# Reading both halves of an input-projection chunk out of their PSUM bank at the chunk's end

## The chip, the cores and the metric

The kernel runs on one core of a Trainium2 chip. The metric is the device time of one execution in microseconds (us); all times here come from the profiled execution or from timed runs of the same program. Engine names are those of the profile: PE multiplies matrices, PEld loads its weights, DVE (VectorE) and ACT (ScalarE) do the element-wise work, POOL is GpSimd, SP issues most transfers.

## What is computed

One layer on 256 tokens of width 1024, in float32: a wide input projection, a recurrent branch (RWKV-7) and a causal attention branch from its columns, a gated mix, a layer norm, and a mixture of 32 experts with the top 4 per token.

```python
proj = x @ w_in                                            # 256 x 5408
sh = token_shift(proj[..., :SHIFT_COLS], mu_shift)         # t + (previous token - t) * mu
y_rwkv = rwkv7_time_mix(r, k, v, ... of sh)
y_attn = moba_attention(q, k, v of proj)                   # rope on q and k, causal softmax
mixed = sigmoid(gate_a) * (y_attn @ w_attn_br) + sigmoid(gate_r) * (y_rwkv @ w_rwkv_br)
h = layer_norm(ALPHA * x + mixed @ w_out)
out = layer_norm(ALPHA * h + moe_ffn(h, ...))              # 32 experts, w1 1024 x 2048, w2 1024 x 1024
```

## The kernel before

**The input projection in chunks and units.** Twenty chunks of 256 columns of `w_in` (numbered 1 to 20) are multiplied with the activations. A chunk's weights come in with one transfer of 1 MB (`load`, L112), and `split` (L121) turns them into a high and a low part with two ACT casts (L128) and two DVE subtractions (L129) of 128x1024 each. A chunk has two halves: of 128 columns each in `proj_shift` and `proj_gate`, of 128 tokens each in `proj_tok`. A half is eight units, one per slice of the contraction, and a unit is three matmuls of 128x256 (`mm3`, L133; lines L135 to L137). So a chunk is 16 units and the projection 320, counted here from 0: chunk c is units 16(c-1) to 16c-1. Both halves lie in one 2 KB PSUM bank, and chunks take banks 0 and 1 in turn.

**How the chunks are read.** Chunks 1 to 6 (k, r, v of the recurrent branch): `shift` (L204), one ACT operation (L205) and one DVE operation (L206) per half. Chunks 7 and 8 (values of attention): one ACT copy per half (L258). Chunks 9 to 12 and 17 to 20 (the two gates): one ACT sigmoid per half (L245). Chunks 13 to 16 (q and k of attention): `rope`, four DVE operations per half (L271, twice L274, L276).

**What sets the order.** PE runs in program order, written by hand. `units()` (L248) is a generator of the 320 units; between the steps of the recurrent branch and of attention the program takes some of them as filler with `fill(n)` or `fill_to(n)`. The order of ACT, DVE, SP and POOL is made by a scheduler when the program is built, and each of these engines then works through its list in order. Waits between engines are placed when the program is built, too.

**The steps around the units that the prediction names**, in program order: the small projections and exponentials of the recurrent branch (L298 to L404); four products that fill the matrices AT (L423), with two units after each; the inversion of triangular blocks on DVE (31 steps, L481 and L483), whose result goes through DRAM and comes back with eight transfers on ACT's queue (L508) for the matmuls of L518 and L526 (after unit 207); the recurrence over four blocks of 64 tokens c = 0 to 3, each a chain of PE and DVE steps (L570, L571, L577, L578, L585, L592, L598, L602) with 10 units between them; two group norms (L538, L551); the transposes of q and k (L626); attention: `scores(0)`, 18 units, `scores(1)`, 12 units, `turn_scores(0)` (L664), units to 313, `weigh(0)` (L677), units to 319. A `scores` step has its softmax on DVE and ACT (exponentials L654, last multiplication L658).

**After unit 319**: the products with the branch and output matrices, the second norm and the router, then a loop over 32 experts whose weights (12 MB each) are streamed by SP (L733) into eleven buffers of 2 MB and one shared with other tiles. A transfer starts when PE has used the buffer's former content (`mdone`). Several of these buffers hold tiles of the projection and of attention before; the transfers of the first experts start when those are done (`mfill`, from L766).

Of the kernel before, what the change touches and what calls it, by code (L numbers as in the profile page):

```python
# [13 lines left out]
AF = mybir.ActivationFunctionType  # L14
# [48 lines left out]
def hybrid_kernel(ctx, tc, xt_d, x_d, win_d, w0_d, ups_d, up2_d, par_d, cA_d, cB_d, wbr_d, wout_d,  # L63
# [7 lines left out]
    V, A, PE, G = nc.vector, nc.scalar, nc.tensor, nc.gpsimd  # L71
# [23 lines left out]
    def bank(i, shape=(512,)):  # L95
        cnt[0] += 1
        return psum.tile([128] + list(shape), FT, name=f"b{i}_{cnt[0]}", tag=f"b{i}")
# [23 lines left out]
    def split(n):  # L121

        if n >= len(chunks):
            return
        hl = pair(hls[n % 3], FR)
        for q in range(2):
            c = slice(1024 * q, 1024 * q + 1024)
            A.copy(hl[:, 0, c], RAW[n][:, c])  # L128
            V.tensor_tensor(hl[:, 1, c], RAW[n][:, c], hl[:, 0, c].bitcast(FT), op=OP.subtract)  # L129
        HL[n] = hl.rearrange("p x (a b) -> p x a b", a=8 if chunks[n][0] == "in" else 4)  # L130
        load(n + 2)

    def mm3(ps, lhs, rhs, first, last):  # L133

        PE.matmul(ps, lhs[0], rhs[0], start=first, stop=False)  # L135
        PE.matmul(ps, lhs[0], rhs[1], start=False, stop=False)  # L136
        PE.matmul(ps, lhs[1], rhs[0], start=False, stop=last)  # L137
# [66 lines left out]
    def shift(dst, ps, mc, m=128):  # L204
        A.activation(dst, ps, AF.Copy, scale=par[:m, P_OM + mc:P_OM + mc + 1])  # L205
        V.scalar_tensor_tensor(dst[:, 1:T], ps[:, 0:T - 1], par[:m, P_MU + mc:P_MU + mc + 1], dst[:, 1:T],  # L206
                               op0=OP.mult, op1=OP.add)
# [7 lines left out]
    def proj_shift(n, b, dst, f0, mc):  # L215
        split(n + 2)
        ps = bank(b, (2, T))
        for h in range(2):
            for kt in range(8):
                mm3(ps[:, h], [HL[n][:, x, kt, 128 * h:128 * h + 128] for x in range(2)], (xh[:, kt], xl[:, kt]),  # L220
                    kt == 0, kt == 7)
                if kt == 7:
                    shift(dst[:, f0 + h], ps[:, h], mc + h)
                yield

    def proj_tok(n, b, done):
        split(n + 2)
        ps = bank(b, (2, 256))
        for tt in range(2):
            tk = slice(128 * tt, 128 * tt + 128)  # L230
            for kt in range(8):
                mm3(ps[:, tt], (xh[:, kt, tk], xl[:, kt, tk]), [HL[n][:, x, kt] for x in range(2)], kt == 0, kt == 7)
                if kt == 7:
                    done(tt, ps[:, tt])
                yield

    def proj_gate(n, b, dst):
        split(n + 2)
        ps = bank(b, (2, T))
        for h in range(2):  # L240
            for kt in range(8):
                mm3(ps[:, h], [HL[n][:, x, kt, 128 * h:128 * h + 128] for x in range(2)], (xh[:, kt], xl[:, kt]),
                    kt == 0, kt == 7)
                if kt == 7:
                    A.activation(dst[:, h], ps[:, h], AF.Sigmoid)  # L245
                yield

    def units():  # L248
        yield from proj_shift(1, 0, k, 0, 4)
        yield from proj_shift(2, 1, k, 2, 6)  # L250
        yield from proj_shift(3, 0, r, 0, 0)
        yield from proj_shift(4, 1, r, 2, 2)
        yield from proj_shift(5, 0, v, 0, 8)
        yield from proj_shift(6, 1, v, 2, 10)

        for half in range(2):
            yield from proj_tok(7 + half, half,
                                lambda tt, ps: A.copy(va_tok[:, tt, 256 * half:256 * half + 256], ps))  # L258
        G_["A"] = slot(15, [8, T])
        for j in range(4):  # L260
            yield from proj_gate(9 + j, j % 2, G_["A"][:, 2 * j:2 * j + 2])
# [18 lines left out]
        for u in range(4):  # L280
            yield from proj_tok(13 + u, u % 2, rope(*divmod(u, 2)))
        G_["R"] = slot(9, [8, T])
        for j in range(4):
            yield from proj_gate(17 + j, j % 2, G_["R"][:, 2 * j:2 * j + 2])
# [59 lines left out]
    for f in range(4):  # L344
        c = slice(128 * f, 128 * f + 128)
        if f % 2 == 0:
            ps = bank(6 + f // 2, (2, T))
# [27 lines left out]
    for f2 in range(2):  # L375
        ps = bank(3 + f2, (2, T))
# [40 lines left out]
    for c in range(4):  # L417
        tt, pr = divmod(c, 2)
# [6 lines left out]
        for h in range(2):  # L425
            ps = pss[h]
# [17 lines left out]
    for c in range(4):  # L444
        ps = bank(2 + c)
# [16 lines left out]
    for tt in range(2):  # L462
        ps = bank(4 + tt)
# [14 lines left out]
    for j in range(31):  # L478
# [5 lines left out]
        if j < 4:  # L484
            c = j
            tt, pr = divmod(c, 2)
            hk, hn = slice(64 * pr, 64 * pr + 64), slice(64 - 64 * pr, 128 - 64 * pr)
            ps = bank(2 + c)
# [72 lines left out]
    for c in range(4):  # L561
        tt, pr = divmod(c, 2)
# [17 lines left out]
        if c < 3:  # L580
            ph = bank(5, (4, 128))
            for s in range(8):
                f, h = s % 4, s // 4
# [12 lines left out]
        for s in range(8):  # L596
            f, h = s % 4, s // 4
# [24 lines left out]
    for f in range(4):  # L622
        ps = bank(6 + f % 2, (2, T))
# [144 lines left out]
    for br, (ys_, gt) in enumerate(((yRs, gR), (yAs, gA))):  # L768
        for cc in range(2):
# [7 lines left out]
            for dd in range(2):  # L777
                d2 = 2 * cc + dd
                ps = bank(2 + d2, (2, T))
# [165 lines left out]
    ps = bank(5, (4, E))  # L945
# [88 lines left out]
    def first(e, b):  # L1034
        j = e % 2
        ps = bank(4 + b)
        pick = misc.tile([128, 128], FR, name="pick", tag="pick")
        A.activation(pick, bo, AF.Copy, scale=dup[:, 2 * e + b:2 * e + b + 1])
        for x in range(2):
            PE.matmul(ps, pick, b1r[:, x], start=x == 0, stop=False)  # L1040
        for kt in range(8):
            w = MW[e, 4 * b + kt // 2]
            for g_ in range(2):
                PE.matmul(ps[64 * g_:64 * g_ + 64], XG[:, kt, 64 * j:64 * j + 64],  # L1044
                          w[:, kt % 2, 512 * g_:512 * g_ + 512], start=False, stop=kt == 7)
            if kt % 2:
                mdone((e, 4 * b + kt // 2))
        return ps
# [32 lines left out]
    for e in range(E):  # L1081
# [6 lines left out]
        ps = first(e, 0)  # L1088
# [125 lines left out]
    with tc.manual_schedule(engines={mybir.EngineType.PE}):  # L1214
        second(E - 2, lambda: turn(E - 1, (1,)))
        for n in range(2):
            ps = [bank(4 + 2 * n + a) for a in range(2)]
# [89 lines left out]
```

## Time and profile before

| | us |
|---|---|
| median of 3 runs (lowest, highest) | 1246.01 (1243.99, 1248.87) |
| profiled execution | 1243.01 |
| its span, first to last instruction | 1241.2 |
| PE, DVE, ACT busy | 1133.4, 387.4, 285.6 |

The profiled execution lies 3.0 us below the median of the runs and has 1.8 us outside its span. Two parts follow each other: the front, up to about 317 us, in which the projection, the two branches and the router run, and the expert loop, from there to the end. In a row of a timeline an idle time and what ended it stand in brackets.

### The profile page before, as it was taken

To read this page: it belongs to the slowest core of one execution; us is meant where nothing else is said; L and a number is where in the kernel's file an instruction comes from. 1 tells how busy PE (TensorE), PEld (TensorE's weight loads), DVE (VectorE), ACT (ScalarE), POOL (GpSimd) and SP (SyncE) were. 2 spreads that over 40 slices of the span, in tenths; PEclk is the share of its full clock that TensorE was granted. 3 is DMA by queue.
4 is the path that set the end of the run, shared out by engine and by line. 5 is a ranking of instruction groups with operands and counts; after the bars stand their busy time and mean duration, and the time that the engine had idled before them with its cause. 6 is when DMAs were issued, how large, how long until landed. Compare 5 with 4: busy or idle time off the path is not lost.

```text
span 1241.2 us, 15213 instructions
## 1 busy us (share of the span) xinstructions
PE 1133.4 (91%) x6434; PEld 596.0 (48%) x6434; DVE 387.4 (31%) x809; ACT 285.6 (23%) x577; POOL 6.5 (1%) x16
## 2 busy tenths in 40 slices
PE   8889887799999999999998989898999999999976
PEld 6678776798444343444433333343343333334322
DVE  4778466465222221222222121211121112222113
ACT  5534325444111111111111111111111111121112
POOL 0000000000000000000000000000000000000000
PEclk9999988899899999999999999999999999999997
DMA  7335423399699999999999999999999999999992
GB/s 269 106 116 156 150 94 145 135 364 380 264 429 427 428 427 429 427 427 418 426 426 430 426 427 429 428 426 428 427 428 427 429 427 428 427 427 427 428 414 87
DMA packets 45549, 441.02 MB, mean 355 GB/s; under 512 B 13010, under 2 KB 13538, under 8 KB 17954
## 3 DMA queue, kind: packets, MB, share of 16 engines
q1 hardware_dynamic: 36002, 436.93, 84.8%
q10 hardware_dynamic: 9472, 3.05, 1.1%
q8 instruction: 52, 0.85, 0.3%
q14 instruction: 23, 0.19, 0.0%
HBM read 438.13 MB, written 1.84 MB: 354 GB/s over the span
## 4 chain that ended last, share of the span: by engine, by line
DMA 49%; PE 41%; DVE 5%; ACT 4%; issue 1%; ACTq 0%; SPq 0%; DVEq 0%
DMA both<-in_w_dram 31%; DMA q<-in_w_dram 16%; PE b L1044 13%; PE b L1027 7%; PE b L135 4%; PE b L137 3%; PE b L136 3%; PE b L914 2%; DVE q L129 1%; PE b L1040 1%; ACT q L128 1%; DMA both<-in_win_dram 1%; PE b L1009 1%; PE b L1064 1%; ACT both L654 1%
## 5 line engine op out<-in xcount | busy, mean ns | idle before, releaser
L1044 PE MATMUL b<-both,s 128*64 128x512 f32 x1280 | 289.8, 600 | 20.4 <-DMA both<-in_w_dram 20.3
L1044 PEld LDWEIGHTS b<-both,s 128*64 128x64 f32 x1280 | 87.8, 138 | 204.7 <-issue 163.2
L1044 PE MATMUL b<-q,s 128*64 128x512 f32 x752 | 171.3, 601 | 4.0 <-DMA q<-in_w_dram 3.8
L1053 DVE TENSOR_SCALAR s<-b 128x256 f32<-128x256 f32 x64 | 27.2, 425 | 440.7 <-PE b L1044 440.7
L1027 PE MATMUL b<-both,s 128*64 128x512 f32 x576 | 128.9, 595 | 3.4 <-DMA both<-in_w_dram 3.4
L135 PE MATMUL b<-q,q 128*128 128x256 f32 x320 | 99.4, 311 | 33.4 <-ACT both L245 15.3
L1027 PE MATMUL b<-q,s 128*64 128x512 f32 x416 | 96.7, 612 | 8.5 <-DMA both<-in_w2l_dram 7.4
L1044 PEld LDWEIGHTS b<-q,s 128*64 128x64 f32 x752 | 51.2, 138 | 107.8 <-issue 97.6
L1069 ACT COPY s<-b 128x256 f32<-128x256 f32 x64 | 23.7, 371 | 323.0 <-PE b L1064 241.1
L137 PE MATMUL b<-q,q 128*128 128x256 f32 x320 | 93.5, 292 | 0.8 <-DVE q L129 0.8
L136 PE MATMUL b<-q,q 128*128 128x256 f32 x320 | 93.5, 292 | 0.0
L1017 DVE TENSOR_TENSOR s<-b,s 64x512 fp32r<-64x512 f32 (+1 forms) x66 | 44.4, 673 | 129.2 <-ACT s L1016 126.8
L135 PEld LDWEIGHTS b<-q,q 128*128 128x128 f32 x320 | 64.3, 201 | 41.0 <-ACT both L245 16.7
L1016 ACT CAST s<-b 64x512 fp32r<-64x512 f32 (+1 forms) x66 | 37.5, 568 | 191.2 <-PE b L1027 178.6
L1027 PEld LDWEIGHTS b<-both,s 128*64 128x64 f32 x576 | 40.4, 137 | 79.5 <-issue 77.8
L914 PEld LDWEIGHTS b<-s,s 128*128 128x128 f32 x512 | 61.7, 200 | 13.8 <-issue 13.0
L914 PE MATMUL b<-s,s 128*128 128x128 f32 x512 | 65.0, 287 | 1.4 <-DVE rt L958 0.7
L137 PEld LDWEIGHTS b<-q,q 128*128 128x128 f32 x320 | 64.3, 201 | 1.0 <-DVE q L129 1.0
L136 PEld LDWEIGHTS b<-q,q 128*128 128x128 f32 x320 | 64.7, 202 | 0.2 <-issue 0.2
L1054 ACT ACTIVATE s<-s 128x256 f32<-128x256 f32 x64 | 27.0, 421 | 143.8 <-DVE s L1053 143.8
L1027 PEld LDWEIGHTS b<-q,s 128*64 128x64 f32 x416 | 29.6, 140 | 62.4 <-issue 59.9
L129 DVE TENSOR_TENSOR q<-both,q 128x1024 fp32r<-128x1024 f32 x44 | 52.5, 1218 | 16.9 <-ACT q L128 16.6
(294 smaller groups left out, 1078.2 us busy)
## 6 DMA issues: line engine op xcount, KB each, us to landing
both<-in_w_dram SPq DMA_DIRECT2D x116, 2048.0 KB, 39.1
q<-in_w_dram SPq DMA_DIRECT2D x73, 2048.0 KB, 39.1
both<-in_win_dram SPq DMA_DIRECT2D x19, 1024.0 KB, 5.1
both<-in_wout_dram SPq DMA_DIRECT2D x4, 1024.0 KB, 7.2
both<-in_w2l_dram SPq DMA_DIRECT2D x7, 512.0 KB, 25.9
s<-in_wbr_dram SPq DMA_DIRECT2D x2, 1024.0 KB, 6.2
both<-in_wbr_dram SPq DMA_DIRECT2D x2, 1024.0 KB, 4.9
s<-in_w_dram SPq DMA_DIRECT2D x2, 1024.0 KB, 16.0
```

The lines of the kernel that those rows point to most:

```text
L129: V.tensor_tensor(hl[:, 1, c], RAW[n][:, c], hl[:, 0, c].bitcast(FT), op=OP.subtract)
L135: PE.matmul(ps, lhs[0], rhs[0], start=first, stop=False)
L136: PE.matmul(ps, lhs[0], rhs[1], start=False, stop=False)
L137: PE.matmul(ps, lhs[1], rhs[0], start=False, stop=last)
L914: PE.matmul(pg[d // 4][:, d % 4], xtok[:, tt, 128 * d:128 * d + 128], oh[:, tt], start=tt == 0 and d % 4 == 0, stop=tt == 1 and d % 4 == 3)
L1016: A.copy(hi, ps)
L1017: V.tensor_tensor(lo, ps, hi.bitcast(FT), op=OP.subtract)
L1027: PE.matmul(ps[64 * n:64 * n + 64], aTs[e % 2][:, b, hf, 64 * g_:64 * g_ + 64], w[:, hf, 512 * n:512 * n + 512], start=ft == 0, stop=ft == 7)
L1044: PE.matmul(ps[64 * g_:64 * g_ + 64], XG[:, kt, 64 * j:64 * j + 64], w[:, kt % 2, 512 * g_:512 * g_ + 512], start=False, stop=kt == 7)
L1053: V.tensor_scalar(gl, pv[:, :, 0], 7.0, None, op0=OP.min)
L1054: A.activation(sw, gl, AF.Sigmoid, scale=1.702)
L1069: A.copy(aTs[e % 2][:, b], ps[:, 2 * i:2 * i + 2])
```

## The change

In all three helpers the reading of half 0 moves from unit 7 of the chunk to unit 15, where half 1 is read too. The condition `h + kt == 8` holds once in a chunk, at h = 1 and kt = 7. The two shifts, and the two calls of `done`, follow each other; the two sigmoids of 128x256 become one of 128x512. No matmul, transfer or buffer changes, and the units are yielded as before.

```diff
@@ proj_shift
-                if kt == 7:
-                    shift(dst[:, f0 + h], ps[:, h], mc + h)
+                if h + kt == 8:
+
+                    for hh in range(2):
+                        shift(dst[:, f0 + hh], ps[:, hh], mc + hh)
                 yield
@@ proj_tok
-                if kt == 7:
-                    done(tt, ps[:, tt])
+                if tt + kt == 8:
+                    for t2 in range(2):
+                        done(t2, ps[:, t2])
                 yield
@@ proj_gate
-                if kt == 7:
-                    A.activation(dst[:, h], ps[:, h], AF.Sigmoid)
+                if h + kt == 8:
+                    A.activation(dst, ps, AF.Sigmoid)
                 yield
```

## Rows read from the trace of the kernel before

**Rows 1.** The chain that ended last, 1150 us to the end: start, us, what
```profile
1162.76 40.83 DMA q<-in_w_dram
```

**Rows 2.** Stretches: busy PE, PEld, DVE, ACT, POOL, then PEclk, DMA share, GB/s
```profile
310.00:320.00 10.00, 9.25 (x47) 7.15 (x47) 2.71 (x14) 1.98 (x5) 0.00 (x0) 0.67 0.53 227
...
340.00:350.00 10.00, 10.00 (x50) 3.44 (x46) 2.01 (x6) 0.98 (x3) 0.00 (x0) 1.00 1.00 429
```

**Rows 3.** Waits of SP, 60 to 400 us: total us, times, longest
```profile
SPq L733 <- PE b L1044: 58.8, 10, 17.8
```

**Rows 4.** The same view, the first 144 us of the front
```profile
0.00:144.00 144.00, 123.52 (x920) 109.39 (x921) 94.27 (x170) 65.94 (x104) 3.62 (x14) 0.98 0.52 164
```

**Rows 5.** Waits of PE, 0 to 144 us: total us, times, longest
```profile
PE b L135 <- DVE both L206: 5.4, 3, 2.2
PE b L135 <- DVE s L206: 3.6, 2, 2.5
PE b L135 <- DVE both L274: 3.2, 1, 3.2
PE b L135 <- ACT both L245: 2.6, 4, 1.2
...
PE b L465 <- DVE s L206: 0.9, 1, 0.9
...
PE b L135 <- ACT both L258: 0.5, 1, 0.5
```

**Rows 6.** Waits of PE, 144 to 201 us
```profile
PE b L135 <- DVE both L274: 4.6, 3, 2.1
PE b L577 <- DVE both L571: 2.8, 1, 2.8
```

**Rows 7.** Waits of PE, 201 to 260 us
```profile
PE b L135 <- ACT both L245: 12.7, 3, 6.1
```

**Rows 8.** Timeline of PE: units 40, two of chunk 18, and unit 280
```profile
47.88 0.39 PE L135 MATMUL b<-q,q 128*128 128x256 f32 x1
...
210.08 0.28 PE L135 MATMUL b<-q,q 128*128 128x256 f32 x1
...
210.44 0.28 PE L135 MATMUL b<-q,q 128*128 128x256 f32 x1
...
217.05 0.58 PE L135 MATMUL b<-q,q 128*128 128x256 f32 x1 [6.09 <-ACT both L245]
```

**Rows 9.** Busy time and granted clock of two stretches (columns as Rows 2)
```profile
170.00:178.00 8.00, 8.00 (x67) 7.59 (x68) 3.03 (x7) 0.82 (x2) 0.00 (x0) 0.58 0.01 2
...
215.00:222.00 7.00, 4.95 (x25) 4.77 (x26) 2.59 (x3) 1.97 (x3) 0.00 (x0) 0.57 0.47 161
```

**Rows 10.** Groups by form, 0 to 260 us: count, busy us, mean ns, idle
```profile
L668 ACT COPY both<-b 128x512 f32<-128x512 f32 x4 | 2.3, 586 | 5.9 <-PE b L664 5.9
...
L206 DVE SCALAR_TENSOR_TENSOR both<-b,par,both 128x255 f32<-128x255 f32 x10 | 4.7, 477 | 8.6 <-ACT both L205 8.5
```

**Rows 11.** Timeline of DVE: a rope half, a step of the recurrence, the softmax's last
```profile
152.35 0.42 DVE L271 TENSOR_TENSOR both<-b,both 128x256 f32<-128x256 f32 x1 [0.21 <-PE b L137]
...
153.20 0.42 DVE L276 TENSOR_TENSOR both<-both 128x256 f32<-128x256 f32 x1
...
183.11 0.67 DVE L571 TENSOR_TENSOR both<-b,both 64x512 f32<-64x512 f32 x1
...
215.24 1.22 DVE L658 TENSOR_TENSOR both<-both,smst 128x1024 f32<-128x1024 f32 x1
```

**Rows 12.** Timeline of ACT around the first softmax
```profile
209.46 1.28 ACT L654 ACT_TABLE_LOAD   x1
...
216.61 0.38 ACT L245 ACTIVATE both<-b 128x256 f32<-128x256 f32 x1
```

**Rows 13.** Timeline: last transfer of the inverse on ACT's queue, first matmul using it
```profile
134.59 0.31 ACTq L508 DMA_DIRECT2D s<-tblk  x1
...
143.67 0.69 PE L518 MATMUL b<-s,s 32*32 32x32 f32 x16
```

## The prediction, made before the result was known

> **What bounds the kernel now.** I read from the end backwards. The chain that ended last closes with weight transfers: one of them alone stands in it for 40.8 us [rows 1], and the busy time of the stretch from 340 us shows the DMA engines full (share 1.00, 429 GB/s) [rows 2]. So from there to the end the time is bytes over bandwidth, and nothing that PE gains inside the expert loop counts. But the stream doesn't run through. Between 310 and 320 us its share is 0.53 [rows 2], because every buffer that is free has been filled and SP waits for PE: the waits of SP name the experts' first product, L1044, ten times, 58.8 us in all [rows 3]. The stream takes off again when PE reaches the first expert. Its start is set by PE at the end of the front, and what PE saves in the front moves the whole stream, and the end, by as much.
>
> In the front PE is the bound: in the first 144 us it is busy 123.5 us, DVE 94.3, ACT 65.9, and DMA has a share of 0.52 [rows 4]. So the question is what PE waits for there. The waits of PE, taken in three stretches, have one pattern above all: L135, the first matmul of a unit, waits for a reader of a chunk, L206, L274, L245 or L258. I add them up:
> - to 144 us: 5.4 + 3.6 + 3.2 + 2.6 + 0.5 = 15.3 us in 11 waits [rows 5]
> - to 201 us: 4.6 us in 3 waits [rows 6]
> - to 260 us: 12.7 us in 3 waits, of which two are about 6.1 [rows 7]
>
> That is 32.6 us in 17 waits. By their place each is unit 8 of a chunk: half 1 is about to be written into the bank from which half 0 is being read. The longest stands at unit 280, for 6.09 us on the gate's sigmoid [rows 8]. That it is the bank and not the unit as such shows at unit 40, where other matmuls lay between the halves: it starts without a wait [rows 8].
>
> **The change part by part.** A unit is 0.36 us at full clock (two L135, one unit apart, at 210.08 and 210.44) [rows 8], so a half is 2.9 us and a chunk 5.8.
>
> *Removed: the wait in the middle of a chunk.* Nothing reads the bank before unit 15 any more, so all 17 go at their places: 32.6 us. Where each then goes I take stretch by stretch.
>
> *Removed with it: slow clock.* Behind three of the longer waits the granted clock is halved, at its 1.2 GHz level. In 215 to 222 us, after the 6.09 us of unit 280, PE is busy 4.95 us at a mean clock of 0.57 [rows 9], nearly all of it at half speed, so 2.4 us are lost; the second such wait, 18 us later, is alike, together 4.8 us. In 170 to 178 us PE is busy throughout at 0.58 [rows 9]: with a share s at half speed, 1 - s/2 = 0.58 gives s = 0.84, 6.7 us, of which 3.4 are lost.
>
> *Moved: the reading of half 0, 8 units (2.9 us) later, in a row with that of half 1.* ACT and DVE do the same work, but a consumer of the chunk right behind its end now has two readings ahead of it instead of one. For a shift that is one L206 more, 0.48 us [rows 10], and its ACT part of the same order; for rope it is 152.35 to 153.62, 1.27 us of DVE [rows 11].
>
> *Merged: eight pairs of gate sigmoids.* Two at 0.38 [rows 12] become one of 128x512, which the trace doesn't show. Its nearest row is the ACT copy of that shape, 0.59 [rows 10]; its bounds are 0.4 (no more than one of today's) and 0.8 (both). I take 0.6. It saves 8 x 0.2 = 1.4 us of an engine that is off the path: nothing.
>
> *To 144 us: 15.3 go, 1.3 come back.* After chunks 2, 4 and 6 (k, r, v) there are 8, 8 and 4 units of cover before their consumer, 2.9, 2.9 and 1.4 us. The last is too short today: the transposes of v wait 0.9 for L206 [rows 5], and one more shift makes that about 1.7. For r I give 0.5. The bounds are 0 and three times a pair of ACT and DVE operations, 2.9. Is there another chain that PE would run into? The inverse of the blocks comes back by transfers on ACT's queue; the last is issued at 134.59 behind the sigmoid of chunk 12, which moves with PE, and PE needs it at 143.67 [rows 13]. In these 9 us there was a wait of 3.2; 5.9 of cover remain. Result 14.0 us.
>
> *144 to 201 us, the recurrence: 4.6 + 3.4 go, 4.0 come back.* Here DVE is itself in the chain. At c = 3 PE already waits 2.8 us for L571 [rows 6], which runs at 183.11 behind a rope half, a split and a norm [rows 11]; a whole chunk of rope ahead of it makes 1.27 more. At c = 1 the second rope half comes ahead of L578 in the same way, 1.27 again. The wait in chunk 16 (4.6/3 = 1.5) I give back wholly: DVE then has the second norm, rope and the branch's output to do in any order, and PE waits for the end of that list. Bounds: 8.0 (all kept) and -1.4 (four ropes late, 5.1; the 1.5; and 2.8 of the clock: 9.4 come back). Result 4.0 us.
>
> *201 to 260 us, attention: 12.7 + 4.8 go, 1.5 come back.* The reason of the two long waits is the order on ACT: the sigmoid of 0.38 us at 216.61 stands behind a table load and 16 exponentials from 209.46 on [rows 12]. PE will now run past it. What is late next? `turn_scores(0)` needs the softmax, whose last operation ends at 215.24 + 1.22 = 216.5 [rows 11]. PE gets there, from unit 280 at 210.8, after 18 units (6.5 us) and `scores(1)`, so not before 217.3: hidden by about a microsecond and the products of `scores(1)`. Then chunk 20 needs the bank that the sigmoid of chunk 18 frees, and `weigh(0)` needs copies on ACT. ACT's block from 209.46 to 217.0 is 7.5 us [rows 12], 16 units are 5.8: each of the two places can cost 1.7, both 3.4. Between 0 and 3.4 I take 1.5. Result 16.0 us.
>
> Sum: 14.0 + 4.0 + 16.0 = 34.0 us. From the profiled execution, 1243.0, that is 1209.0; its own time lies 3.0 under the median, so I forecast 1212 for the median. The added bounds, 15.3 + 8.0 + 17.5 = 40.8, give 1205.
>
> **The rivals.**
>
> *A. The lists of ACT and DVE give a third back.* They are made anew by the scheduler, and their order isn't in the trace. For it: L571 stands behind a split that nobody awaits soon [rows 11]. Against: DVE has a third of its time free [rows 4]. Price: the recurrence keeps nothing, attention keeps its waits without 3.4 and without the clock (12.7 - 3.4 = 9.3), the first stretch 12.4: 21.7 us, 1224.
>
> *B. The bank comes free too late.* Chunk n + 2 writes the bank of chunk n, 5.8 us after its end. If the sigmoid of chunk 18 is put behind the second softmax, it waits for that block of 7.5 us [rows 12], which waits for DVE first, for one operation like L658 at least, 1.2 [rows 11]: 8.7 less 5.8 is 2.9 us at the start of chunk 20, and a slow stretch of 2.4 like that of [rows 9] follows. 34.0 - 5.3 = 28.7, 1217. Against: chunk 18 ends before the second scores are there, so ACT would stand idle with the sigmoid ready. The Trainium skill ("PSUM — Partial Sum Buffer", Summary: rules for kernel authors) says to evacuate promptly, as PSUM is tight; the change does the opposite. By that rule this rival would be the likely one; the trace so far bears out only half of it, since two alternating banks leave 5.8 us for the reading.
>
> *C. Slower: the readers, not the bank, are the bound.* The 17 waits end with the reader; if DVE and ACT were the bound in the front, all 32.6 us would come back at the chunk's end or at a consumer. The deferred reading would then cost itself: three shift pairs (2.9), four ropes (5.1) and one more slow stretch (2.4) make 10 us, 1256. It decides from the point where DVE's list has no idle time left in the stretch; it is busy 94 of 144 us [rows 4], so only the recurrence comes near.
>
> *D. It doesn't do what it says.* If something else that ends with the reading held unit 8 (the subtraction of a split on the same DVE, say), PE would wait there still, and the time would stay, 1246. Against: unit 40 [rows 8], and that gates are read by ACT alone and show the same wait.
>
> **How the numbers follow.** Forecast (1205 to 1221 by its own bounds, 40.8 and 12.4 - 1.4 + 14.1 = 25.1) 0.57, A 0.25, B 0.10, C 0.04, D 0.04. The time is the forecast's, 1212. The range takes in B, A and half of what A could grow to, 1204 to 1232, and leaves out C, D and the tail of A. Half a per cent, about what a measurement of this kernel can tell from no change, is 6.2 us; faster than 1240 are forecast, B and nearly all of A, 0.91; within it D and a rest of A, 0.05; slower C, 0.04.
>
> **What would show it.** Right: no wait of L135 for L206, L245, L258 or L274 that is longer than a few tenths; the first product of expert 0 (L1044) some 34 us earlier; the granted clock at full speed where [rows 9] show 0.57; the stream's dip moved along with it, and the same time as before from the dip to the end. The steps apart: the wait of L465 at 1.4 to 1.9, of L571 at 3 to 5, that of L664 and L677 under 2. Wrong: waits of equal sum at L577, L664 or L677; a wait of L135 at the start of a chunk (B); or L1044 earlier while the end stays, which would say that the stream isn't started by PE.

## The result, and the profile after

The changed kernel takes 1208.4 us (median of 3 runs, 1206.2 to 1208.9) against 1246.0; the ratio is 0.969 with an interval of 0.965 to 0.972. Its profiled execution takes 1208.9 us and has a span of 1207.1, 34.1 less than that of before. Line numbers behind the three helpers are 3 higher than before: L1047 is the first product of an expert (L1044 of before), L426 the product of L423, L468 the transposes of v, L580 and L574 the steps L577 and L571, L558 and L552 the steps L555 and L549, L248 the gate's sigmoid.

The starts of five steps on PE, from the traces of all kernels that were run (line numbers of before; "rest" is the span less the start of the first expert product):

```
               L423   L518   L626  L677   L1044    span    rest
before         67.2  143.7  198.9  244.6  317.7   1241.2  923.5
after          65.2  132.2  186.5  214.2  285.2   1207.1  921.9
e1_shift       61.9  134.4  188.7  235.7  308.6   1230.7  922.1
e2_tok         70.9  143.5  197.8  243.8  316.9   1238.7  921.8
e3_gate        68.7  139.1  197.3  225.9  296.9   1219.2  922.3
e4_mid         70.2  143.7  196.2  239.6  309.4   1232.9  923.5
e5_banks       62.7  129.3  186.4  217.9  288.3   1211.8  923.5
e6_two_sig     63.6  129.1  183.0  210.7  280.4   1202.7  922.3
e7_front_pad   60.3  141.3  195.3  222.9  292.6   1215.1  922.5
e8_loop_pad    59.8  126.7  180.7  208.4  278.3   1203.0  924.7
e9_pool_split  63.0  130.0  185.5  213.1  282.9   1205.1  922.2
e10_again      63.6  130.6  185.0  212.6  283.6   1205.6  922.0
e11_mix        60.8  124.5  174.5  203.1  272.9   1195.0  922.1
```

Of the 34.1 us, 11.5 are gained up to L518, 0.9 from there to L626, 18.0 from there to L677, 2.1 up to the first expert and 1.6 behind it.

The waits of PE in the changed kernel, to 144 us and from there to 201 us (columns as in [rows 5]); the same view from 201 to 260 us has no row at all, where [rows 7] had 12.7 us:

```profile
PE b L426 <- DVE s L410: 2.2, 1, 2.2
PE b L468 <- DVE s L206: 1.6, 1, 1.6
PE b L135 <- ACT q L128: 1.3, 1, 1.3
...
PE b L558 <- DVE both L552: 3.4, 1, 3.4
PE b L580 <- DVE both L574: 3.1, 1, 3.1
PE b L573 <- DVE s L596: 1.5, 1, 1.5
PE b L558 <- issue: 1.3, 1, 1.3
```

Not one of the 17 waits of L135 for a reader of [rows 5 to 7] is left (the one for L128 is the first chunk's split at the start). What stands there instead are waits of the consumers, 2.2 and 1.6 us behind r and v, and four in the recurrence.

Three stretches of the changed kernel by busy time (columns as [rows 2]): attention, the dip of the weight stream, and after it:

```profile
186.50:214.20 27.70, 27.46 (x213) 25.75 (x211) 17.13 (x22) 19.39 (x38) 0.00 (x0) 1.00 0.34 120
...
285.00:290.00 5.00, 5.00 (x26) 1.65 (x26) 0.73 (x4) 1.42 (x4) 0.00 (x0) 1.00 0.22 64
310.00:320.00 10.00, 10.00 (x59) 5.12 (x59) 2.67 (x7) 1.10 (x4) 0.00 (x0) 1.00 0.99 423
```

In attention PE is busy throughout at full clock, where [rows 9] had 0.57. The dip of the stream has moved with the first expert product, and SP's next transfer is issued 3.7 us behind the start of that product, as before (321.4 after 317.7):

```profile
285.21 1.08 PE L1047 MATMUL b<-both,s 128*64 128x512 f32 x4
```
```profile
288.91 0.33 SPq L736 DMA_DIRECT2D both<-in_w_dram  x1
```

### The profile page after: what moved, and what is told of

It reads as the page before. It is cut to its first block, busy times and chain, and to the rows that moved or that the text cites. A ratio compares the mean times of both kernels' runs of the same rounds, so it can differ in the third digit from the quotient of the medians.

```text
span 1207.1 us, 15203 instructions
## 1 busy us (share of the span) xinstructions
PE 1127.8 (93%) x6434; PEld 592.1 (49%) x6434; DVE 386.0 (32%) x809; ACT 283.4 (23%) x569; POOL 6.5 (1%) x16
## 5 line engine op out<-in xcount | busy, mean ns | idle before, releaser
L1047 PE MATMUL b<-both,s 128*64 128x512 f32 x1280 | 290.9, 602 | 17.9 <-DMA both<-in_w_dram 17.6
L1047 PEld LDWEIGHTS b<-both,s 128*64 128x64 f32 x1280 | 88.4, 138 | 202.4 <-issue 165.5
L1047 PE MATMUL b<-q,s 128*64 128x512 f32 x752 | 172.7, 606 | 2.4 <-DMA q<-in_w_dram 2.3
L1047 PEld LDWEIGHTS b<-q,s 128*64 128x64 f32 x752 | 51.7, 139 | 107.0 <-issue 100.1
L135 PE MATMUL b<-q,q 128*128 128x256 f32 x320 | 97.4, 304 | 1.3 <-ACT q L128 1.3
L135 PEld LDWEIGHTS b<-q,q 128*128 128x128 f32 x320 | 64.5, 201 | 5.9 <-issue 2.9
```

## The experiments

The theory: a matmul into a bank that is being read waits for the reader, PE is the bound of the front, and the first expert product starts the weight stream, so each microsecond that PE saves in front of it is a microsecond at the end. The rivals are that the readers are the bound (C), that the half's boundary and not the bank makes the wait (D), and that the gain has another source. Each was run beside the kernel before (1243.7 to 1244.3 us on these chips).

**One helper at a time.** Each of these has the new condition in one helper only, as the diff of the change has it:

```diff
# e1_shift: proj_shift alone      # e2_tok: proj_tok alone      # e3_gate: proj_gate alone
-                if kt == 7:
+                if h + kt == 8:
```

> Only the shifts (chunks 1 to 6) are read at the chunk's end; rope, copies and gates as before. Theory (PE waits at unit 8 for the bank, and what it saves in the front moves the end): the waits of L135 for L206, 9.0 us, are gone, those for L245 and L274 stand; some of it comes back at the products after r and v, as in the changed kernel (2.2 at L426, 1.6 at L468 there), so 6 us faster, 3 to 9. Rival (readers are the bound): all comes back at L423 and L465, 0 to 3 us slower. Over all three single parts the theory expects gains that add up to that of the whole change, 34 to 38 us.

Measured: 1232.5 us against 1244.2, ratio 0.991 (0.988 to 0.993), 11.7 us faster. The waits for L206 are gone, those for the gates stand at 15.3, and the two consumers' waits of the changed kernel are here already:

```profile
PE b L135 <- ACT both L247: 15.3, 7, 6.1
...
PE b L425 <- DVE s L409: 2.2, 1, 2.2
PE b L467 <- DVE s L206: 1.6, 1, 1.6
```

The direction is the theory's; the size is beyond its 3 to 9 us. Two things were not in that sum: what a stop of PE costs beyond its row (below, in e4: by an estimate 1.4 us for the five), and the wait of unit 200, which the edit does not touch. Before, rope's first operation there is followed on DVE by two subtractions of a split, and PE waits 3.19 us; in e1 the list is another, and PE waits 0.91. The DVE rows of before, then PE's in e1:

```profile
137.46 0.42 DVE L271 TENSOR_TENSOR both<-b,both 128x256 f32<-128x256 f32 x1 [5.64 <-PE b L137]
137.80 2.35 DVE L129 TENSOR_TENSOR q<-both,q 128x1024 fp32r<-128x1024 f32 x2
```
```profile
131.32 0.39 PE L135 MATMUL b<-q,q 128*128 128x256 f32 x1 [0.91 <-DVE both L276]
```

> Only the token-major chunks (7, 8 and the rope chunks 13 to 16) are read at the chunk's end. Theory: the waits of L135 for L274 and L258, 8.3 us, are gone; the 3.7 before the recurrence stay gained, of the 4.6 in it most comes back at L571, L555 and L570 where DVE is in the chain: 6 us faster, 3 to 9. Rival (deferred rope holds up the recurrence): the step from the first matmul of L518 to that of L626 gets longer than before by 1 to 5 us, and the whole is within 2 us of before.

Measured: 1239.0 us, ratio 0.995 (0.994 to 0.997), 5.1 us faster, as the theory had it. The step from L518 to L626 takes 54.3 us against 55.2 before: 4.6 us of waits went, and L555 (L556 here) now waits 3.4 for the second norm behind the rope:

```profile
PE b L556 <- DVE both L550: 3.4, 1, 3.4
```

The recurrence gets no longer by the deferred rope, and hardly shorter.

> Only the gates (chunks 9 to 12 and 17 to 20) are read at the chunk's end. Theory: the waits of L135 for L245, 15.3 us, are gone, and with them the two slow-clock stretches behind the waits of 6.1 us (4.8): 20 us faster, 17 to 23, the largest of the three parts. Rival (the two long waits were the softmax's own time): PE waits for it at the transposes of the scores instead, and the gain is 3 to 8 us.

Measured: 1217.5 us, ratio 0.977 (0.973 to 0.980), 26.7 us faster, the largest part, and more than the 17 to 23 expected; the profiled execution, the slowest of its four, is 22 us shorter than that of before. Unit 200 waits 0.91 us here too. In the trace the step from L626 to L677 falls from 45.7 to 28.6 us. The softmax is not what PE had waited for: from 200 to 255 us one wait of 0.8 us is left, for a copy of the transposed q and k.

```profile
PE b L626 <- ACT both L627: 0.8, 1, 0.8
```

The three gains make 43.5 us, the whole change 36 to 38. Part of the excess shows in the traces: the 3.2 us of unit 200 go in e2, and 2.3 of them go in e1 and in e3 as well, so they are counted more than once. The intervals (3.6, 1.9 and 4.3 us to a side) are too wide to settle the rest.

**Reading in the middle of half 1.**

```diff
-                if kt == 7:                       # gate and tok alike
-                    shift(dst[:, f0 + h], ps[:, h], mc + h)
+                if h and kt in (3, 7):
+                    hh = kt // 4
+                    shift(dst[:, f0 + hh], ps[:, hh], mc + hh)
```

> Half 0 is read four units into half 1 (behind unit 11), half 1 at the chunk's end, all three helpers. Theory (the bank: a matmul into a bank that is being read waits, wherever it stands): the 17 waits move from unit 8 to unit 12 and keep their length, so the time is that of before within 6 us. Rival (it is the start of a half, or reading later as such, that costs or helps): no waits in the middle, and the time of the changed kernel, 34 to 38 us faster than before.

Measured: 1231.1 us, ratio 0.988 (0.984 to 0.992), 13.1 us faster. The place is what the theory said: every wait of L135 for a reader now stands at unit 12 of its chunk, none at unit 8, and units 44 and 108 have one too, whose chunks had none before because other matmuls lay between their halves; chunk 5 has lost its own, since other matmuls (L423) now lie in front of its unit 12. The length is not: they add up to 23.1 us instead of 32.6.

```profile
PE b L135 <- ACT both L246: 9.7, 7, 4.7
PE b L135 <- DVE both L206: 5.8, 4, 2.5
PE b L135 <- DVE both L275: 4.2, 4, 1.5
...
PE b L135 <- DVE s L206: 2.5, 1, 2.5
...
PE b L135 <- ACT both L259: 0.9, 2, 0.5
```

So it is the matmul into the bank that waits, wherever it stands, and rival D falls. That a wait keeps its length holds where the reader is free (0.47 us for a gate, as before). Where it is busy it was wrong: the wait ends when the reader's list is through, and PE comes four units later. The long ones are 4.65 and 2.73 us instead of 6.09 and 6.10. The first is shorter by 1.44 us, which is four units: its sigmoid starts 17.7 us after the first L626 in both kernels. The second is shorter by more; what else moved there was not traced.

The same trace shows what one stop of PE costs. These are the last matmul of unit 139 and the first two of unit 140:

```profile
114.99 0.28 PE L137 MATMUL b<-q,q 128*128 128x256 f32 x1
115.74 0.38 PE L135 MATMUL b<-q,q 128*128 128x256 f32 x1 [0.47 <-ACT both L246]
115.97 0.28 PE L136 MATMUL b<-q,q 128*128 128x256 f32 x1
```

From start to start this is 0.75 and 0.23 where a running stream has 0.12 and 0.12: 0.74 us are lost, and the row shows 0.47 of them. The rest, 0.27, is the end of the matmul before, which otherwise lies under the next one, and the slower start.

**A bank for each half, read as early as before.**

```diff
-        ps = bank(b, (2, T))
+        ps = [bank(0, (T,)), bank(1, (T,))]      # half h is written to and read from ps[h], at its kt == 7
```

> Each half has a bank of its own (half 0 bank 0, half 1 bank 1, in every chunk), and each is read at its end, as before the change. Theory (the bank): a half's bank is wanted again 8 units, 2.9 us, after the reading can start, so waits of up to 2.9 us vanish, and of the two of 6.1 us and the one of 3.2 some 3.2, 3.2 and 0.3 stay: 6.7 of 32.6 stay, and shorter waits leave less slow clock: 28 us faster, 20 to 36. Rival (reading at the half as such is the cause, in whatever bank): the waits stay, and the time is that of before within 6 us.

Measured: 1209.5 us, ratio 0.971 (0.968 to 0.974), 34.2 us faster, and the same as the changed kernel within its runs. The half is read where it was read before the change; only the bank is another (and with it the tile, since each half is now a tile of its own), and PE's waits for the readers fall from 32.6 to 7.1 us:

```profile
PE b L135 <- ACT both L245: 3.7, 3, 2.3
PE b L135 <- DVE both L206: 3.4, 2, 2.1
PE b L555 <- DVE both L549: 2.6, 1, 2.6
PE b L577 <- DVE both L571: 2.0, 1, 2.0
```

With that the cause is shown from the other side: not when the half is read, but that PE's next half lay in the same bank. One thing stays open: these waits are semaphores that are placed when the program is built, and bank and tile change together in this run. Two tiles within one bank were not tried, so the runs don't tell a wait for the bank from a wait for the tile, and they say nothing of what the chip would do without the semaphore. Rival C falls too, since the readers do the same work in both.

**Two sigmoids at the chunk's end instead of one.**

```diff
-                    A.activation(dst, ps, AF.Sigmoid)
+                    for hh in range(2):
+                        A.activation(dst[:, hh], ps[:, hh], AF.Sigmoid)
```

> The changed kernel with two sigmoids of 128x256 at the chunk's end instead of one of 128x512. Theory: the merging saves 1.4 us of ACT, which is off the path: the time of the changed kernel within 2 us. Rival (fewer, larger instructions are where the gain comes from): 5 to 20 us slower than the changed kernel.

Measured: 1207.1 us (1204.5 to 1211.2), ratio 0.971 (0.969 to 0.974): the changed kernel. The merged sigmoid takes 0.60 us, the value taken (its row stands in the account of attention below), and the merging is worth nothing that shows.

**The same PE work, in the front and in the loop.** Both are the changed kernel with some 14 us of matmuls more, whose results are overwritten by the next one.

```diff
# e7_front_pad, proj_gate, ahead of the first unit of chunk 11
+                for _ in range(117 if (n, h, kt) == (11, 0, 0) else 0):
+                    PE.matmul(ps[:, 0], HL[n][:, 0, 0, 0:128], xh[:, 0], start=True, stop=True)
# e8_loop_pad, first(), once in each of the 64 calls
+        PE.matmul(ps, pick, b1r[:, 0], start=True, stop=True)
```

> The changed kernel with 117 more matmuls of 128x256 at the start of chunk 11, whose results are overwritten: 14 us of PE work in the front at 0.12 each. Theory (the front's end on PE starts the weight stream): the first product of expert 0 and the end are both 14 us later, 12 to 15: some 1222. Rival (the stream is bound by bytes from earlier on): the end moves by less than 5 us.

> The changed kernel with one more matmul of 128x512 in front of each of the 64 first products of the expert loop, its result overwritten: 64 x 0.22 = 14 us of PE work in the loop. Theory (there the end is set by the weight transfers): the end within 2 us of the changed kernel. Rival (PE bounds the loop too, busy nine tenths of it): 10 to 14 us later.

Measured: 1220.0 us (0.982; 0.979 to 0.984) with the work in the front, 1208.4 us (0.971; 0.970 to 0.973) with it in the loop. In the front it costs 12 to 13 us, in the loop nothing by the medians. For the front the comparison is with e6 and e8, run beside it: its first expert product starts at 292.6 us, against 280.4 and 278.3. Against the earlier profile of the changed kernel (285.2) it is only 7.4 later; profiles of the same front differ by nearly that much (278.3 to 285.2; the last section says what goes with it). In the loop most of the added work went into PE's waits for the weights: L1047 (L1048 with the added line) waited 17.6 us for transfers, and 8.3 with the added work, 9.3 of the 14 us. The first fence is the changed kernel, the second e8.

```profile
PE b L1047 <- DMA both<-in_w_dram: 17.6, 17, 2.0
```
```profile
PE b L1048 <- DMA both<-in_w_dram: 8.3, 7, 1.2
```

That is the step of the prediction that carries everything else, and the table above says it for all kernels: the rest lies between 921.8 and 924.7 us in 13 traces whose first expert product starts anywhere from 272.9 to 317.7. The 924.7 are those of e8, so of its 14 us some 2 to 3 do show there.

**Taking work off DVE in the recurrence.** Beside the changed kernel itself, run again:

```diff
-            V.tensor_tensor(hl[:, 1, c], RAW[n][:, c], hl[:, 0, c].bitcast(FT), op=OP.subtract)
+            (G if n in (17, 18) else V).tensor_tensor(hl[:, 1, c], RAW[n][:, c], hl[:, 0, c].bitcast(FT), op=OP.subtract)
```

> The changed kernel as it is, beside the two that follow, on one chip: 1208 us within 3. Its front up to L423 began at 59.8 to 65.2 us in four profiles of kernels that are the same up to there; one more value of that spread is wanted.

> The changed kernel with the subtractions (L129) of chunks 17 and 18, four of 1.2 us on DVE in the recurrence, on POOL, which is idle there. Theory (DVE's list is the bound in the recurrence: the 3.1 us at L577 and the 3.4 at L555 of the line numbers of before are waits for operations behind those subtractions): these two waits shrink by 1.2 to 2.4 each, 3 us faster than the changed kernel, 1 to 5. Rival (the chain of PE and DVE steps itself, or POOL disturbing DVE): both waits stay, or DVE's operations get longer, 0 or slower.

Measured: 1207.9 us (0.971; 0.969 to 0.973) for the changed kernel, 1207.2 us (0.971; 0.968 to 0.973) with the subtractions on POOL. The rival was right. POOL takes 4.9 us for two, and while it works, an addition of rope that takes 0.41 us otherwise takes 1.68 (DVE, then POOL, in e9):

```profile
162.78 0.42 DVE L274 TENSOR_TENSOR both<-b,both 128x256 f32<-128x256 f32 x1
...
163.78 1.68 DVE L279 TENSOR_TENSOR both<-both 128x256 f32<-128x256 f32 x1
```
```profile
162.79 4.87 POOL L129 TENSOR_TENSOR q<-both,q 128x1024 fp32r<-128x1024 f32 x2 [12.27 <-ACT q L128]
```

L274 has one input in PSUM and keeps its 0.42; L279 has two inputs in SBUF. The Trainium skill ("SBUF — State Buffer", Who interferes with whom) says that a DVE instruction with two SBUF inputs contends with a GpSimd instruction that reads SBUF; these rows agree. So whether DVE's list bounds the recurrence was not decided by this run: the work left DVE, and the time came back in its other operations. The waits at L577 and L555 stay, 3.8 and 3.5 us.

**Gates at the chunk's end, all else early with a bank for each half.**

```diff
# proj_shift and proj_tok as in e5_banks (read at each half's end, half h in bank h)
# proj_gate as in the change (one bank in turn, one sigmoid at the chunk's end)
```

> Gates at the chunk's end as in the changed kernel; shifts, copies and rope read at each half's end as before, but with a bank for each half. Theory (the bank; whether the reading is early or late matters little once PE doesn't wait): no long waits of L135 for L245; the waits at the products after r and v (2.2 and 1.6) and of rope's list in the recurrence become waits at unit 0 or 8 for a late reading (3.4 with a bank for each half): within 4 us of the changed kernel. Rival (early reading is worth it for the consumers): 4 to 8 us faster.

Measured: 1196.8 us (1196.6 to 1198.8), ratio 0.962 (0.960 to 0.964), 47.4 us faster than before and 11.1 faster than the changed kernel on the same chip. The rival was right, and by more than it had said. Its waits:

```profile
PE b L135 <- DVE both L206: 3.4, 2, 2.1
PE b L555 <- DVE both L549: 2.6, 1, 2.6
PE b L577 <- DVE both L571: 2.0, 1, 2.0
```

The gain over e10_again lies up to L518 (6.1 us) and in the recurrence (4.4); attention takes 1.0 us more, and the step behind it 1.2 less. The waits alone don't make it. The clock helps: two stretches of e10_again, then the same two of e11 (columns as [rows 2]):

```profile
0.00:130.60 130.60, 122.72 (x910) 109.60 (x910) 90.29 (x163) 62.76 (x97) 3.61 (x14) 0.96 0.53 172
130.60:185.00 54.40, 45.18 (x506) 42.54 (x506) 40.49 (x84) 18.57 (x24) 0.00 (x0) 0.91 0.49 176
```
```profile
0.00:124.50 124.50, 118.36 (x910) 105.97 (x910) 90.83 (x167) 62.83 (x97) 3.61 (x14) 1.00 0.55 180
124.50:174.50 50.00, 43.70 (x505) 41.07 (x505) 39.11 (x80) 17.62 (x23) 0.00 (x0) 0.93 0.54 190
```

PE does the same matmuls up to L518 in 118.4 busy us at a clock of 1.00, where it needed 122.7 at 0.96; 4.4 of the 6.1 us are busy time. In the recurrence e5 reads shifts and rope just as e11 does, has the same waits there (2.6 and 2.0), and is slower than the changed kernel, at a clock of 0.79:

```profile
129.30:186.40 57.10, 50.76 (x504) 47.74 (x505) 37.52 (x77) 19.02 (x24) 0.00 (x0) 0.79 0.47 159
```

So the 4.4 us of the recurrence can't be put down to the early reading. That the whole of e11 is 11 us faster holds over its five runs; how much of that the early reading brings, by sparing PE stops, and how much is where the slow stretches fall, was not separated.

## Why the prediction was right, point by point

- **The end is set by the start of the weight stream, and that by PE**: shown. The first expert product is 32.5 us earlier, the end 34.1; 14 us more on PE cost 12 to 13 in the front and at most 2 to 3 in the loop.
- **The 17 waits are the bank's**: shown, by e4 (the waits follow the read to unit 12) and e5 (another bank, the same early reading, and 25.5 of 32.6 us go). Open is only whether it is the bank or the tile that the program guards, since no run has two tiles in one bank.
- **The first stretch, 14.0 forecast, 11.5 in the profile.** The cover of r was mis-sized: 0.5 us was given for the product behind it, and L426 waits 2.2. The working had one more L206 in the way; in fact ACT's new list has two casts of a later split between the two shifts of chunk 4, and DVE's list has a subtraction of that split in front of L410, the operation that L426 waits for.

```profile
60.19 0.47 ACT L205 ACTIVATE both<-b,par 128x256 f32<-128x256 f32 x1 [2.70 <-PE b L137]
60.56 1.99 ACT L128 CAST q<-both 128x1024 fp32r<-128x1024 f32 x2
62.45 0.48 ACT L205 ACTIVATE both<-b,par 128x256 f32<-128x256 f32 x1
```
```profile
63.36 1.22 DVE L129 TENSOR_TENSOR q<-both,q 128x1024 fp32r<-128x1024 f32 x1
```

  The second shift waits 2 us for casts that nobody needs yet. The wait behind v came out as said, 1.6. Two more terms were not in the sum, and about cancel: the slow clock is longer than before here (a mean of 0.95 against 0.98), which differs between profiles of the same instructions, as the last section shows; on the other side the 11 stops were worth more than their rows, by an estimate from the one measured in e4 (0.27 us each) 3 us. PE is busy 123.2 us up to L518 in both kernels, and all of the 11.5 is idle time.
- **The recurrence, 4.0 forecast, 0.9 to the transposes of q and k.** The step that failed is the wait of chunk 16, given back at 1.5 us: the transposes of L555 wait 3.4 us for the second norm, whose last operation stands on DVE behind rope and a subtraction (first fence), and those of the first norm another 1.3. L571's 3.1 us were in the range named (3 to 5), and the product after it at c = 2 waits 1.5. These are the same with rope alone deferred (e2), so they are the price of that part. A second term was mis-sized: the 3.4 us of slow clock that were to go with the wait of unit 232. They went in part only. PE's busy time for the same work falls by 2.1 us, and the clock is 0.91 on average where it was 0.88 (second fence, before and after); between 170 and 178 us of the changed kernel it is 0.68, with PE busy throughout. So the slow clock did not hang on that wait alone.

```profile
179.36 1.22 DVE L129 TENSOR_TENSOR q<-both,q 128x1024 fp32r<-128x1024 f32 x1
...
180.91 0.68 DVE L552 TENSOR_TENSOR both<-both,gst 128x512 f32<-128x512 f32 x1
```
```profile
143.70:198.90 55.20, 47.17 (x505) 43.80 (x505) 35.50 (x77) 17.15 (x22) 0.00 (x0) 0.88 0.41 144
132.20:186.50 54.30, 45.09 (x505) 42.44 (x505) 40.50 (x84) 18.54 (x24) 0.00 (x0) 0.91 0.50 175
```

- **Attention, 16.0 forecast, 18.0.** The two waits of 6.1 us went with the slow clock behind them, and nothing came back: not at the softmax, and neither at chunk 20's bank nor at `weigh(0)`, for which 1.5 had been set aside. ACT takes the sigmoid as soon as chunk 18 ends (its last matmul ends at 203.57), with 16 units to spare: rival B had no chance to begin.

```profile
203.61 0.60 ACT L248 ACTIVATE both<-b 128x512 f32<-128x512 f32 x1
```

- **The total** was right by more than its parts were: 2.5 and 3.1 us too much in the first two stretches, 2.0 too little in the third, and 3.7 behind it that were not in the sum (2.1 up to the first expert product and 1.6 behind it, which is within the spread of the 13 traces). The slow stretch in the router's part is 6.8 us long instead of 10.2, which can account for most of the 2.1. That such misses cancel is luck. The median came out 3.6 us under the 1212 for another reason: the 3.0 us added for it came from three runs, and over more runs (7 to 14) the median of before is 1243.7 to 1244.3, close to the profiled 1243.0.

Of the rivals, A was half right in kind: the lists gave back some 9 us of waits in the first two stretches, and the stops' hidden cost, which A didn't know either, paid for a part of it. C, by which the front couldn't get shorter, is refuted by e5, and D by e4.

## What to carry to other kernels

Where two results share a PSUM bank, as the halves of a chunk do here, the program lets PE begin the second only when the first has been read. Where the reader is free the wait is about the read itself (0.47 us for a gate's sigmoid of 0.38); where it isn't, the wait is the reader's list (6.1 us for the same sigmoid behind the exponentials). Look for the first matmul into a bank with a reader as releaser; either give each result its own bank and read it early, or read both at the end, whichever leaves the consumer its cover: here a mix of the two measured best, the deferred reading where nobody waits for the result (the gates), the second bank where a chain does (shifts and rope), though how much of its lead is the clock stays open. Before counting such a gain, ask what starts the stage that sets the end: here a transfer that waits for PE's first use of a buffer.

## What the runs showed of the hardware

- A stop of PE costs more than the idle time in its row: 0.74 us from start to start where the row has 0.47, measured at one stop between matmuls of 128x256 at full clock.
- The granted clock can fall to its 1.2 GHz level though PE was not idle just before. In the profile of the changed kernel it does so near 31.8 us, in the seventh of eight pairs of matmuls that follow each other without a gap, every other pair over 32 rows only. PE had been busy for 15.0 of the 15.2 us up to there at full clock. Three of the pairs, from the timeline of PE (start, busy us, engine, line):

```profile
31.00 0.69 PE L352 MATMUL b<-both,both 32*128 32x256 f32 x2
31.63 1.12 PE L351 MATMUL b<-both,both 128*128 128x256 f32 x2
32.67 1.22 PE L352 MATMUL b<-both,both 32*128 32x256 f32 x2
```

  A pair takes 0.7 us ahead of the fall and 1.1 to 1.2 from there on. The time before the fall and the slow stretch, from the busy time by windows of the same kernel (columns as in [rows 2]):

```profile
16.60:31.80 15.20, 14.96 (x99) 11.71 (x100) 9.64 (x17) 12.97 (x26) 0.00 (x0) 1.00 0.70 243
31.80:38.60 6.80, 6.80 (x26) 5.50 (x27) 4.63 (x4) 5.96 (x8) 0.00 (x0) 0.50 0.32 101
```

  In the profile of e8 the same matmuls take 0.7 us a pair to the end. Five kernels that are the same up to there (after, e6, e7, e8, e10) reach L423 at 59.8 to 65.2 us, a spread of 5.4 us in the first twentieth of the span. It goes with the clock: the mean up to L423 is 1.00 in e7 and e8 (60.3 and 59.8 us), 0.95 in e6 and e10 (63.6 both) and 0.92 in the changed kernel (65.2). What makes the clock fall in one profile and not in another was not tried.
- In attention the clock goes with PE's long waits. The four kernels that keep the long waits of the gates there (before, e1, e2, e4) have a mean clock of 0.80 to 0.85 between L626 and L677; the other nine have 1.00.
- A DVE addition with both inputs in SBUF went from 0.41 to 1.68 us beside a subtraction on POOL; one with an input in PSUM did not change.
